# Two short runs of unread TensorE products in a hybrid decoder layer: while the first tokens load, and between the two products of the feed forward

## The chip, the cores and the metric

The kernel runs on one core of a Trainium2 chip. The metric is the device time of one execution in microseconds (us). Engines are named as in the profile: PE is TensorE, DVE is VectorE, ACT is ScalarE, POOL is GpSimd, SP is the engine that issues most of the transfers.

## The reference, cut to what matters

```python
def reference(x, w_in, w_o, ..., w_up, w_down, ln2_g, ln2_b):    # x: 1024 tokens x 1024, float32
    proj = x @ w_in[l]
    q, k, v, iq, ik, iw, hq, hf, hi, hg = jnp.split(proj, _split_points(), axis=-1)
    ...
    att = dsa_attention(q, k, v, iq, ik, iw * idx_w_scale)       # top 256 keys of each query by the indexer
    hgo = hgrn2(hq, hf, hi, hg, lower_bounds[l], hg_norm_g[l])   # gated linear recurrence
    mix = jnp.concatenate([att, hgo], axis=-1) @ w_o[l]
    x = layer_norm(ALPHA * x + mix, ln1_g[l], ln1_b[l])
    h = jnp.square(jax.nn.relu(x @ w_up[l])) @ w_down[l]         # 1024 -> 4096 -> 1024
    x = layer_norm(ALPHA * x + h, ln2_g[l], ln2_b[l])
```

## The kernel before

Every large product is made at float32 precision out of three faster ones: both operands are split into a high part (ACT, L88) and the rest (DVE or POOL, L89), and `mm3` issues high x high, high x low and low x high (L123 to L125) into one PSUM bank. PSUM is cut into three groups of banks: "mm" (four), "tr" (two) and "ou" (two).

The order in which the program writes the work is not the order in which the engines do it. The kernel is built with a planner (`schedule_with_timeline_sim`, L39): it plays the instructions through against estimated durations and writes the queue of each engine from that. Each engine then takes its queue strictly in that order.

*The start.* `turn_x(t)` (L144 to L151) loads 128 tokens (`xn`, 512 KB), transposes them on PE in eight 128x128 steps (L150, against `ident`) into "tr" banks, and splits them into `XH` and `XL`. The loads of tokens 0 and 1 are issued first, then four loads of the first weights (`wraw`, 324 columns), then the other tokens. The first products that mean something (`natural`, for the indexer, 128x324) follow from these tokens and weights. SBUF tiles `score[0..5]` (the indexer's scores) are reserved here, and first written much later by DVE.

*The middle.* Projections, the top-k search on DVE (`reach`, L313, and its rounds), the recurrence (`hgrn_unit`), attention, the output projection and the first layer norm.

*The feed forward.* Both products are done by a scheme of seven products for eight blocks. The first one runs over `NP` = 16 pairs of column blocks: `start_pair` issues two of a pair's seven `product`s and `end_pair` five, and the results go to memory (`hs`, `hd`). After the last `end_pair` the pools of the first product are closed, and the second product takes their place in SBUF: `down_w` and `down_h` load `rb` (weights) and `rs` (the stored results) and split them into `tw` and `sh`; `down_chunk` multiplies them (L123 to L125 with `tw`, `sh`), and DVE adds each finished bank to `acc` (L1072, L1074). SBUF is handed over tile by tile (`reuse_waits="tile"`): a load may start when the last reader of the tile that lay there is done.

Of the kernel before, what the change touches and what calls it, by code (L numbers as in the profile page):

```python
# [21 lines left out]
P = 128  # L22
# [20 lines left out]
def layer(ctx, tc, x, w_in, w_o, lb_logits, hg_norm_g, ln1_g, ln1_b, w_up, w_down, ln2_g, ln2_b,  # L43
          rope_tab, turn_tab, ident_c, causal_c, level_c, block_c, out, probe=None):
    nc = tc.nc
    PE, ACT, DVE, POOL = nc.tensor, nc.scalar, nc.vector, nc.gpsimd

    def dma(dst, src):
        return nc.sync.dma_start(dst, src)  # L49
# [18 lines left out]
    def bank(tag, bufs, shape=(P, 512), name="ps"):  # L68
        return psum.tile(list(shape), F32, name=name, tag=tag, bufs=bufs)

    def mm_bank(shape=(P, 512)):
        return bank("mm", 4, shape)

    def tr_bank(shape=(P, 4, P)):
        return bank("tr", 2, shape)
# [4 lines left out]
    ident = base.tile([P, P], F32, name="ident")  # L80
# [5 lines left out]
    def split_out(hi, lo, src, eng=None):  # L86

        first = ACT.activation(hi, src, AF.Copy)  # L88
        (eng or DVE).tensor_tensor(lo, src, hi.bitcast(F32), op=OP.subtract)  # L89
        return first  # L90
# [31 lines left out]
    def mm3(ps, ah, al, bh, bl, first, last, **kw):  # L122
        PE.matmul(ps, ah, bh, start=first, stop=False, **kw)  # L123
        PE.matmul(ps, ah, bl, start=False, stop=False, **kw)  # L124
        PE.matmul(ps, al, bh, start=False, stop=last, **kw)  # L125


    XH = [xt_tile(), xt_tile()]
# [4 lines left out]
    score = [s_pool.tile([P, P * (3 + j)], F32, name=f"score{j}") for j in range(6)]  # L133
# [10 lines left out]
    def turn_x(t):  # L144
        xn = xp.tile([P, DM], F32, name="xn", bufs=5)
        dma(xn, x[t * P:(t + 1) * P, :])
        for g in range(2):
            ps = tr_bank()
            for i in range(4):
                PE.transpose(ps[:, i], xn[:, (4 * g + i) * P:(4 * g + i + 1) * P], ident)  # L150
            split_out(XH[t // 4][:, t % 4, 4 * g:4 * g + 4, :], XL[t // 4][:, t % 4, 4 * g:4 * g + 4, :], ps)  # L151
# [7 lines left out]
    def natural(segs, evac, ws=None):  # L159

        n = sum(b - a for a, b in segs)
        ws = ws or in_weights(segs)
        for pr in range(4):
            ps = [mm_bank((P, n)) for _ in range(2)]
            for k in range(NK):
                w = ws[k // 2]
                for i in range(2):
                    t = 2 * pr + i
                    mm3(ps[i], XH[t // 4][:, t % 4, k, :], XL[t // 4][:, t % 4, k, :],
                        w[:, 0, k % 2, :], w[:, 1, k % 2, :], k == 0, k == NK - 1)  # L170
            for i in range(2):
                evac(2 * pr + i, ps[i])
            yield

    def turned(c0, dst):

        ws = [weight([rows(w_in, c0, c0 + 512, 2 * kp, 2)], [2, 512], 1, halves=True) for kp in range(4)]
        for g in range(2):
            for i in range(2):
                ps = [mm_bank() for _ in range(2)]  # L180
                for k in range(NK):
                    w = ws[k // 2]
                    for b in range(2):
                        sl = slice((2 * b + g) * P, (2 * b + g + 1) * P)
                        mm3(ps[b].rearrange("p (t n) -> p t n", t=4), w[:, 0, k % 2, sl], w[:, 1, k % 2, sl],
                            XH[i][:, :, k, :], XL[i][:, :, k, :], k == 0, k == NK - 1)
                n = slice(i * 512, (i + 1) * 512)
                for b in range(2):
                    u = kq.tile([P, 512], F32, name="ru", bufs=2)
                    v = kq.tile([P, 512], F32, name="rv", bufs=2)  # L190
                    DVE.tensor_tensor(u, ps[b], tab[:, 0, n], op=OP.mult)
                    DVE.tensor_tensor(v, ps[1 - b], tab[:, 1, n], op=OP.mult)
                    POOL.tensor_tensor(u, u, v, op=OP.add if b else OP.subtract)
                    parts = kq.tile([P, 2, 512], F32R, name="rparts", bufs=2)
                    split_out(parts[:, 0], parts[:, 1], u)
                    for j in range(2):
                        dma(dst[j, 4 * g:4 * g + 4, b, :, n], parts[:, j].bitcast(F32))
                yield
# [17 lines left out]
    first, irs = [], {}  # L216
# [23 lines left out]
    def turn_idx(t):  # L240
# [4 lines left out]
        if t >= 2:  # L245
# [4 lines left out]
            ACT.activation(iqs[:, :, sq], tp, AF.Copy)  # L250
            DVE.tensor_tensor(iqs[64:, :, sq], tp[64:], iqs[64:, :, sq].bitcast(F32), op=OP.subtract)

    turn_x(0)
    turn_x(1)
    ws = in_weights([(CI, CI + NI)], 2, xp)
# [541 lines left out]
    last = pairs[3]["last"]  # L797
# [48 lines left out]
    BX = {}  # L846
# [31 lines left out]
    for half in range(2):  # L878
        cs_ = slice(half * 512, half * 512 + 512)
        ws = [weight([rows(w_o, half * 512, half * 512 + 512, 2 * kp, 2)], [2, 512], 1, after=last) for kp in range(4)]  # L880
        for prt in range(4):
            ps = [mm_bank() for _ in range(2)]
# [23 lines left out]
    for tt in range(4):  # L906
        a, b = X1[tt], X1[tt + 4]
# [14 lines left out]
    def weights(p):  # L922
        r = raw_up(p, 2 * P)
        if p >= PRE:
            first_weights(p, r)
        a11, a12, a21, a22 = r[:, :4, :P], r[:, 4:, :P], r[:, :4, P:], r[:, 4:, P:]
        s = [upp.tile([P, 4, P], F32, name="ws", bufs=4) for _ in range(4)]
        DVE.tensor_tensor(s[0], a21, a22, op=OP.add)
        DVE.tensor_tensor(s[1], s[0], a11, op=OP.subtract)
        wq_split(p, "s2", s[1])  # L930
        wq_split(p, "s1", s[0])
        DVE.tensor_tensor(s[2], a11, a21, op=OP.subtract)
        wq_split(p, "s3", s[2])
        DVE.tensor_tensor(s[3], a12, s[1], op=OP.subtract)
        wq_split(p, "s4", s[3])
        wq_split(p, "22", a22)

    def product(ps, p, a, b, first):

        w = wq.pop((p, a))  # L940
        for k in range(4):
            mm3(ps, w[:, 0, k], w[:, 1, k], BX[b][:, 0, k], BX[b][:, 1, k], first and k == 0, k == 3,
                skip_group_check=True)

    def copied(ps):
        e = upp.tile([P, 512], F32, name="e", bufs=4)
        ACT.activation(e, ps, AF.Copy)
        return e
# [4 lines left out]
    def h_tile():  # L953
        return upp.tile([P, 512], F32, name="h", bufs=9)

    def keep(p, name, h):
        c = next(i for i, r in enumerate(CHUNKS) if p in r)
        ACT.dma_start(hs_d[c][ORDER.index(name), p - CHUNKS[c][0]], h)

    def block(p, i, j, ps, e=None):  # L960

        h = h_tile()
        if e is not None:
            DVE.tensor_tensor(h, ps, e, op=OP.add)
        ACT.activation(h, ps if e is None else h, AF.Relu)
        ACT.activation(h, h, AF.Square)
        if p in PLAIN:
            ACT.dma_start(hd[p][i * P:(i + 1) * P, j * 512:(j + 1) * 512], h)
            return
        name = f"a{j + 1}{i + 1}"  # L970
        hb[p, name] = h
        if name != "a21":
            keep(p, name, h)
        sums = {"a21": (("s1", "a21", "a22", OP.add), ("s2", "s1", "a11", OP.subtract), ("s3", "a11", "a21", OP.subtract)),
                "a12": (("s4", "a12", "s2", OP.subtract),)}
        for n, x1, x2, op in sums.get(name, ()):
            hb[p, n] = h_tile()
            DVE.tensor_tensor(hb[p, n], hb[p, x1], hb[p, x2], op=op)
            keep(p, n, hb[p, n])

    def start_pair(p):
        X = mm_bank()
        product(X, p, "11", "11", True)
        e1 = copied(X)
        Y = ou_bank()
        product(Y, p, "12", "21", True)
        block(p, 0, 0, Y, e1)
        held[p] = X

    def end_pair(p):  # L990
        X = held.pop(p)
        product(X, p, "s2", "t2", False)
        e2 = copied(X)
        Z = mm_bank()
        product(Z, p, "s1", "t1", True)
        e5 = copied(Z)
        product(X, p, "s3", "t3", False)
        block(p, 1, 1, X, e5)
        product(Z, p, "s4", "22", False)
        block(p, 0, 1, Z, e2)  # L1000
        product(X, p, "22", "t4", False)
        block(p, 1, 0, X)

    for p in range(PRE):
        start_pair(p)
    for p in range(NP):
        weights(p)
        if p >= PRE:
            start_pair(p)
        end_pair(p)  # L1010
    es_v.close()
    es_u.close()
    es_c.close()
# [101 lines left out]
    for t in range(NT):  # L1115
        ts = slice(t * P, (t + 1) * P)
        for gs in G:
            ps = mm_bank()
# [47 lines left out]
```

## Time and profile before

| | us |
|---|---|
| median of 3 runs | 1383.96 (1382.64 to 1385.42) |
| the profiled execution | 1383.45 |
| its span, first to last instruction | 1381.70 |
| PE busy | 1310.3 (95%) |
| DVE busy | 968.9 (70%) |
| ACT busy | 594.3 (43%) |
| POOL busy | 371.4 (27%) |

The mean granted clock of PE is 0.976 of full speed. PE's share is high nearly throughout; what matters are the few stretches where it is not. The records of matmuls have ends that are modelled, and they overlap: the distance from one start to the next says how fast PE goes, not the length of a record.

### The profile page before, as it was taken

The numbers are of one execution on the slowest core, as the hardware profiler recorded it, in microseconds if no ns is written. First come the engines' busy times: TensorE is split into PE (matmuls) and PEld (weight loads), VectorE is DVE, ScalarE is ACT, GpSimd is POOL, SyncE is SP. The second block draws the span as 40 slices with busy tenths as digits, with TensorE's granted clock in tenths as the row PEclk, the third lists the DMA queues.
The fourth block names the chain that finished last, engine by engine and source line by source line (L and its number), as shares of the span: only waits on it lengthen the run. The fifth ranks groups of instructions, "written<-read, shape, count | busy, mean of one in ns | idle before, by whom it ended". The sixth has DMA issues, their size and how long they took to land. (4 is left out here: it accounts for less than half of the span.)

```text
span 1381.7 us, 20797 instructions
## 1 busy us (share of the span) xinstructions
PE 1310.3 (95%) x7961; PEld 1067.1 (77%) x7961; DVE 968.9 (70%) x1821; ACT 594.3 (43%) x1038; POOL 371.4 (27%) x344
## 2 busy tenths in 40 slices
PE   8999799889899999999998999999998899999996
PEld 8877678677679956667887888888886688888875
DVE  4557989999993345553378755566537999887568
ACT  3333346655522455562135655555545343333131
POOL 3433302434515201132482000000003442341016
PEclk9999899999999999999999999999999999999998
DMA  5333322101103294106322544434466554443123
GB/s 219 111 101 104 101 57 61 45 20 32 48 32 92 72 192 99 36 31 199 128 99 79 176 145 160 160 130 151 154 213 240 187 196 149 157 160 92 54 100 122
DMA packets 96948, 162.50 MB, mean 118 GB/s; under 512 B 5832, under 2 KB 41040, under 8 KB 96720
## 3 DMA queue, kind: packets, MB, share of 16 engines
q1 hardware_dynamic: 81584, 133.37, 31.1%
q10 hardware_dynamic: 15264, 27.79, 5.7%
q8 instruction: 63, 1.03, 0.3%
q14 instruction: 37, 0.30, 0.1%
HBM read 114.48 MB, written 46.66 MB: 117 GB/s over the span
## 5 line engine op out<-in xcount | busy, mean ns | idle before, releaser
L123 PE MATMUL ps<-tw,sh 128*128 128x512 f32 x392 | 154.3, 396 | 8.5 <-ACT tw L88 5.1
L123 PE MATMUL ps<-w,xt 128*128 128x512 f32 (+2 forms) x448 | 158.4, 358 | 3.1 <-ACT HI L430 1.8
L125 PE MATMUL ps<-w,xt 128*128 128x512 f32 (+2 forms) x448 | 159.1, 356 | 0.0
L124 PE MATMUL ps<-w,xt 128*128 128x512 f32 (+2 forms) x448 | 158.9, 356 | 0.0
L124 PE MATMUL ps<-tw,sh 128*128 128x512 f32 x392 | 154.4, 394 | 1.5 <-DVE tw L89 1.5
L125 PE MATMUL ps<-tw,sh 128*128 128x512 f32 x392 | 153.0, 394 | 0.2 <-DVE sh L89 0.2
L89 POOL TENSOR_TENSOR w<-wraw,w 128x1024 fp32r<-128x1024 f32 (+2 forms) x46 | 95.5, 2087 | 118.5 <-ACT w L88 115.7
L1052 POOL TENSOR_TENSOR tt<-rb,rb 128x1536 f32<-128x1536 f32 (+1 forms) x5 | 19.6, 3912 | 392.1 <-DVE tw L89 314.7
L1074 DVE TENSOR_TENSOR acc<-acc,ps 128x512 f32<-128x512 f32 x140 | 92.0, 678 | 35.6 <-PE ps L125 35.5
L88 ACT ACTIVATE sh<-rs 128x1536 fp32r<-128x1536 f32 (+1 forms) x35 | 49.1, 1403 | 151.6 <-PE ps L125 141.7
L123 PE MATMUL ps<-xt,w 128*128 128x512 f32 x256 | 102.9, 402 | 0.0
L313 DVE TENSOR_SCALAR_CACHE_REDUCE junk<-score,cand 128x384 uint8<-128x384 f32 (+1 forms) x124 | 100.4, 810 | 2.7
L124 PE MATMUL ps<-xt,w 128*128 128x512 f32 x256 | 101.9, 398 | 0.0
L125 PE MATMUL ps<-xt,w 128*128 128x512 f32 x256 | 101.6, 397 | 0.0
L124 PE MATMUL ps<-xt,wq 128*128 128x512 f32 x256 | 99.9, 390 | 0.0
L123 PE MATMUL ps<-xt,wq 128*128 128x512 f32 x256 | 99.7, 390 | 0.0
L125 PE MATMUL ps<-xt,wq 128*128 128x512 f32 x256 | 99.6, 390 | 0.0
L345 ACT ACTIVATE sjunk<-score,scand 128x896 int8<-128x896 f32 (+1 forms) x62 | 67.8, 1094 | 69.5 <-DVE scand L355 53.5
L123 PEld LDWEIGHTS ps<-w,xt 128*128 128x128 f32 x448 | 86.0, 193 | 15.0 <-ACT HI L430 2.2
L124 PEld LDWEIGHTS ps<-w,xt 128*128 128x128 f32 x448 | 86.1, 192 | 11.5 <-issue 0.8
L123 PEld LDWEIGHTS ps<-tw,sh 128*128 128x128 f32 x392 | 75.0, 192 | 25.8 <-ACT tw L88 5.5
L125 PEld LDWEIGHTS ps<-w,xt 128*128 128x128 f32 x448 | 86.1, 192 | 10.4
(240 smaller groups left out, 3074.2 us busy)
## 6 DMA issues: line engine op xcount, KB each, us to landing
hs<-h ACTq DMA_DIRECT2D x98, 256.0 KB
rs<-hs SPq DMA_DIRECT2D x28, 768.0 KB
wr<-in_w_up_dram SPq DMA_DIRECT2D x16, 1024.0 KB
rb<-in_w_down_dram SPq DMA_DIRECT2D x16, 768.0 KB
wraw<-in_w_in_dram SPq DMA_DIRECT2D x20, 512.0 KB
ks<-kd SPq DMA_DIRECT2D x16, 512.0 KB
xn<-in_x_dram SPq DMA_DIRECT2D x8, 512.0 KB
kd<-rparts SPq DMA_DIRECT2D x16, 256.0 KB
```

What stands on the lines that cost most here:

```text
L88: first = ACT.activation(hi, src, AF.Copy)
L89: (eng or DVE).tensor_tensor(lo, src, hi.bitcast(F32), op=OP.subtract)
L123: PE.matmul(ps, ah, bh, start=first, stop=False, **kw)
L124: PE.matmul(ps, ah, bl, start=False, stop=False, **kw)
L125: PE.matmul(ps, al, bh, start=False, stop=last, **kw)
L313: DVE.tensor_scalar(junk[:, :wide[j]], score[j], at, 0.0, op0=op, op1=OP.add, accum_out=res)
L345: ACT.activation(sjunk[:, :wide[NB + j]], score[NB + j], AF.Sign, bias=0.0 if bias is None else bias[:, j:j + 1], scale=1.0, accum_out=cnt ...
L1052: POOL.tensor_tensor(t1, b12, b11, op=OP.subtract)
L1074: DVE.tensor_tensor(acc[t][:, gs], acc[t][:, gs], ps, op=OP.add)
```

## The change

A helper `keep_busy(n, m, after)` takes one "tr" bank and issues `n` products of a 128x128 float32 tile with itself. Nothing reads the bank. Each product is put behind `after` in the planner's order, without a wait of its own. It is called twice: with 8 products of a part of `score[0]`, which DVE fills with zeros for it, ahead of the first `turn_x`; and with 15 products of `ident` behind the last product of the first half of the feed forward. The other edits only return the last instruction, so that it can be named.

```diff
     def mm3(ps, ah, al, bh, bl, first, last, **kw):
         PE.matmul(ps, ah, bh, start=first, stop=False, **kw)
         PE.matmul(ps, ah, bl, start=False, stop=False, **kw)
-        PE.matmul(ps, al, bh, start=False, stop=last, **kw)
+        return PE.matmul(ps, al, bh, start=False, stop=last, **kw)
+
+    def keep_busy(n, m, after):
+
+        ps = tr_bank((P, P))
+        for _ in range(n):
+            r = PE.matmul(ps, m, m, start=True, stop=True)
+            tc.add_manual_dep(r.ins, after.ins.name, mybir.DependencyInfo(
+                mybir.DependencyClass.NoSync, mybir.DependencyReason.SCHED_ONLY), reason="place in the order")
...
+    keep_busy(8, score[0][:, :P], DVE.memset(score[0][:, :P], 0.0))
     turn_x(0)
     turn_x(1)
...
-        product(X, p, "22", "t4", False)
+        end = product(X, p, "22", "t4", False)
         block(p, 1, 0, X)
+        return end
...
-        end_pair(p)
+        end = end_pair(p)
+    keep_busy(15, ident, end)
     es_v.close()
```

## Rows read from the trace of the kernel before

**Rows 1.** Busy time and granted clock by stage (stretch, length, engines, PEclk, DMA share, GB/s).
```profile
4.75:11.20 6.45, 5.89 (x24) 5.40 (x25) 3.95 (x6) 4.82 (x8) 1.57 (x1) 1.00 1.03 382
11.20:30.00 18.80, 18.80 (x136) 18.75 (x136) 10.65 (x25) 5.48 (x13) 8.65 (x7) 1.00 0.60 224
...
200.00:390.00 190.00, 172.99 (x2124) 139.92 (x2123) 185.81 (x546) 104.91 (x210) 76.45 (x116) 0.96 0.14 39
...
740.00:1039.10 299.10, 299.10 (x1306) 244.92 (x1305) 178.70 (x275) 160.66 (x279) 0.00 (x0) 1.00 0.47 157
```

**Rows 2.** Instructions of PE in order of time, start of the kernel.
```profile
4.75 1.94 PE L150 MATMUL ps<-ident,xn 128*128 128x128 f32 x8 [4.75 <-DMA xn<-in_x_dram]
...
9.17 0.62 PE L124 MATMUL ps<-w,xt 128*128 128x324 f32 x1
...
11.21 0.36 PE L124 MATMUL ps<-w,xt 128*128 128x324 f32 x1
11.41 0.31 PE L125 MATMUL ps<-w,xt 128*128 128x324 f32 x1
11.56 0.31 PE L123 MATMUL ps<-w,xt 128*128 128x324 f32 x1
...
15.70 1.03 PE L150 MATMUL ps<-ident,xn 128*128 128x128 f32 x8
```

**Rows 3.** All engines in order of time, start of the kernel.
```profile
0.79 0.10 DVE L341 MEMSET need<- 128x1 f32 x2 [0.79 <-PEq L1155]
...
5.88 0.60 ACT L88 ACTIVATE xt<-ps 128x512 fp32r<-128x512 f32 x1 [3.88 <-PE ps L150]
6.50 0.69 DVE L89 TENSOR_TENSOR xt<-ps,xt 128x512 fp32r<-128x512 f32 x1 [5.62 <-ACT xt L88]
...
8.01 0.83 DVE L89 TENSOR_TENSOR w<-wraw,w 128x648 fp32r<-128x648 f32 x1
...
10.40 0.74 ACT L88 ACTIVATE w<-wraw 128x648 fp32r<-128x648 f32 x1
```

**Rows 4.** One line's durations (minimum, median, maximum in ns).
```profile
L150 PE MATMUL ps<-ident,xn x64: 270/273/474, 4.8 to 40.1; 128*128 128x128 f32 x64
```

**Rows 5.** PE in order of time: four float32 products, recorded as eight passes.
```profile
521.38 1.05 PE L751 MATMUL ps<-ident,wide 128*128 128x128 f32 x8
```

**Rows 6.** PE in order of time between the two products of the feed forward.
```profile
1038.73 0.39 PE L125 MATMUL ps<-xt,wq 128*128 128x512 f32 x1
1044.19 2.08 PE L123 MATMUL ps<-tw,sh 128*128 128x512 f32 x4 [5.07 <-ACT tw L88]
```

**Rows 7.** Busy time and granted clock there, columns as in rows 1.
```profile
1039.10:1042.20 3.10, 0.01 (x1) 0.00 (x0) 0.25 (x1) 2.28 (x3) 0.00 (x0) 0.99 0.73 246
1042.20:1044.20 2.00, 0.01 (x1) 0.01 (x1) 1.01 (x2) 1.06 (x1) 0.00 (x0) 0.50 0.86 293
1044.20:1049.00 4.80, 4.80 (x11) 3.80 (x12) 2.98 (x3) 1.06 (x1) 1.78 (x1) 0.50 1.04 394
1050.80:1094.10 43.30, 38.14 (x153) 29.77 (x152) 43.30 (x36) 20.66 (x18) 24.76 (x7) 0.92 0.61 207
1081.00:1086.30 5.30, 5.28 (x12) 4.15 (x13) 5.30 (x5) 1.76 (x2) 2.70 (x1) 0.50 0.49 148
```

**Rows 8.** The chain of waits there (start us, us, what ran or was waited for).
```profile
1039.14 0.38 SPq L49
...
1041.99 9.05 DMA rs<-hs
...
1089.90 4.15 DVE sh L89
...
1094.09 0.50 PE ps L125
1094.59 0.23 PE ps L123
```

**Rows 9.** From the page: a costly group of DVE (count, busy us, mean ns).
```profile
L313 DVE TENSOR_SCALAR_CACHE_REDUCE junk<-score,cand 128x384 uint8<-128x384 f32 (+1 forms) x124 | 100.4, 810 | 2.7
```

More of the change, by code (lines that the diff above doesn't have):

```diff
@@ L941, in product @@
         for k in range(4):
-            mm3(ps, w[:, 0, k], w[:, 1, k], BX[b][:, 0, k], BX[b][:, 1, k], first and k == 0, k == 3,
-                skip_group_check=True)
+            r = mm3(ps, w[:, 0, k], w[:, 1, k], BX[b][:, 0, k], BX[b][:, 1, k], first and k == 0, k == 3,
+                    skip_group_check=True)
+        return r
     def copied(ps):
```

## The prediction

> **What bounds the kernel now.** I read the busy time and clock by stage first. From 11.2 to 30 us PE is busy all of the time, and again over 299 us from 740 to 1039; in the stretch from 200 to 390 us DVE is the fuller engine, 185.8 us of 190 [rows 1]. So time that PE gains in the first microseconds reaches the end if what comes after is released by PE's own work. Then I read PE in order of time at the start. Its first instruction waits 4.75 us for the first tokens. After that it runs at half rate: seven starts of 128x324 products lie between 9.17 and 11.21, 0.29 us each, and then the distance falls to 0.15 us [rows 2]. [...] The transposes agree: eight at 4.75 take 1.94 us and eight at 15.70 take 1.03 us [rows 2].
>
> At the second place PE starts its last product of the first half at 1038.73 and waits 5.07 us from its end to 1044.19 [rows 6]. The clock is granted in full to about 1042.2, half from there to 1049.0; in that half-rate stretch eleven 128x512 products start in 4.80 us, 0.436 us each, against 0.23 us in the chain later [rows 7, 8]. But the chain of waits here does not run over PE. It goes from SP's issue at 1039.14 over the load of the stored results (9.05 us) and then, among DVE's splits and additions, to a last split that ends at 1094.05, for which PE waits at 1094.09 [rows 8]. DVE is busy 43.30 of 43.30 us from 1050.8 to 1094.1, PE only 38.14 [rows 7]. The reader is to see two places with the same symptom, a slow PE, and a different engine on the path.
>
> **The eight products at the start.** What they cost: a float32 product is recorded as two passes; eight passes took 1.05 us at the full clock [rows 5], the last record about 0.27, so (1.05 - 0.27)/7 = 0.111 us a pass. At half rate the transposes give the price: (1.94 - 0.47)/7 = 0.21 us a record, the last one being the longest of its line [rows 2, 4]. Sixteen passes take 3.4 to 3.6 us. They wait for the zeros: DVE's first instruction starts at 0.79, and DVE is idle until 6.50 [rows 3], so the fill is hidden there; I estimate 0.2 to 0.3 us for it from the small fill of 0.10 us, and a start at 1.1 to 1.2 us. They end at 4.5 to 4.8, against 4.75 when the tokens are in. Delay: 0 to 0.1 us.
>
> What they give: from PE's first work to the rise of the clock it took 6.45 us at the start (4.75 to 11.2) and 4.8 and 5.3 us in the two slow stretches later [rows 2, 7]. From 1.15 that puts the rise at 6.0 to 7.6 us instead of 11.2. Up to 11.14 ACT sets the pace, not PE: it is busy 4.82 us of the stretch's 6.45 and its conversions run from 5.88 to the one at 10.40, nearly without a gap [rows 1, 3]. So faster transposes bring nothing. The products after them gain. DVE has the low part of the first weights at 8.84 [rows 3]; the product at 9.17 could start at 8.9, and the seven to 11.21 would take 7 x 0.15 = 1.05 in place of 2.04 us [rows 2]. That is 1.0 + 0.27 = 1.3 us at most. Some of these products, in a fixed order, will stand for a low part that POOL or DVE has not yet made, so I take 0.9 us. The bounds are 0 (the clock does not rise, or the inputs hold PE) and 1.3; half of PE's 5.89 busy us would be 2.9, and ACT's fill excludes that. The next thing in the way is the second pair of token tiles: their transposes at 15.70 show no wait [rows 2], so the loads were in; that they were in 0.9 us earlier is not shown, and if not the gain ends there. I carry 0.9 us to the end, as PE is full to 30 us and the later stages hang on its products.
>
> **The fifteen products.** Thirty passes of 0.111 us are 3.3 us: from 1039.1 to 1042.4, before 1044.19, when PE's next operand is ready [rows 5, 6]. They are hidden by that wait, with 1.7 us to spare. If the clock were down they would take 6.3 us and end at 1045.4, 1.2 us too late. PE's idle time falls from 5.07 to 1.7 us, and the clock had held for some 3 us after the last product [rows 7], so I expect it to stay up: PE gains 11 x 0.2 = 2.2 us by 1049. What is late next is the load: DVE's full stretch begins when the stored results have landed and ACT has converted them, and it ends the wait at 1094.09. So I carry 0 of the 2.2 us; bounds 0 and 2.2, nearer 0 by the row in which DVE has no idle time at all. The loads are issued when the last real product ends; the fifteen read only `ident` and write a bank, so they hold up none of them. A second slow stretch, from 1081 to 1086 [rows 7], follows a wait for DVE and stays.
>
> **The other edits** return a value and cost nothing. The sum: 1383.45 - 0.9 - 0 = 1382.55 for the profiled execution. The median of the runs shown lies 0.51 above it, so 1383.96 - 0.9 = 1383.1. About 0.2% (2.8 us) is what a measurement here can tell from no change, and this is a third of it.
>
> **Rivals.**
>
> *The second place pays as well.* If the planner now puts three of DVE's four additions of the first product ahead of the split at 1050.8, in the time in which DVE waits for the load, PE's 2.2 us are kept: 0.9 + 2.2 = 3.1, 1380.9. For it: PE and DVE end within 0.1 us of each other at 1094 [rows 8]. Against it: DVE's order must change, for which I see no cause there.
>
> [...]
>
> *The planner's order turns out dearer.* All queues are written by playing the whole program through; the trace shows that this moves work far (fills that the program writes in the middle run at 0.79 [rows 3]). Eight products at the start and fifteen later shift that play. The place where it costs most is the stretch from 200 to 390 us, where DVE is full: a round of the search, four counts of 0.81 us [rows 9], put ahead of a step that PE waits for, costs 3.2 us. One such round gives 1383.1 + 3.2 = 1386.3, two 1389.5; it decides from 2.8 + 0.9 = 3.7 us, a little more than one round. For it: nothing keeps the order fixed. Against it: the shift is small.
>
> *The planner's order turns out cheaper*, by the same round: 1383.1 - 3.2 = 1379.9.
>
> **How the numbers follow.** My forecast has 0.40, the unraised clock 0.14, both within 0.2%. The second place paying has 0.20 and the cheaper order 0.11, both faster; the dearer order has 0.15, of which I count 0.13 as slower. That makes faster 0.31, same 0.56, slower 0.13. The range goes from the cheaper order with some of the second place's gain (1379.3) to one dear round (1386.5); the likeliest case's own range is 1382.5 to 1384.1.
>
> **What would show it.** Right: sixteen passes before the first transpose, which still starts within 0.1 us of 4.75; 128x324 products 0.15 us apart before 9.5 us; the transposes of 15.70 at about 14.8; the clock at 1.00 from 1039 to 1077 and thirty passes in the gap; DVE's full stretch and PE's wait at its end about where they were, counted from the last real product. Wrong: distances of 0.27 us to 11 us; the first `sh`-and-`tw` stretch ending over 1 us sooner after that product; or a gap between the two traces that grows in the middle of the kernel, where neither place lies.

## The result, and the profile after

| | median, us | ratio to before (95% interval) |
|---|---|---|
| before, on the same chip | 1382.64 (1380.52 to 1387.16) | |
| the change | 1375.37 (1372.3 to 1378.3, and one of 2953.8) | 0.9942 [0.992, 0.9964] |
| the change once more, with profile | 1376.68 (1372.89 to 1378.61) | 0.9946 [0.9928, 0.9964] |

The kernel is faster by some 7 to 8 us. 1383.1 was forecast, with a range from 1379.3: the direction that had got 0.31 came true, with eight to nine times the gain forecast, and the range missed it. The profiled execution of the change took 2953.8 us, over twice the others; the ratio leaves it out, and the profile of the third row is shown, with a span of 1376.7 us.

By stage, columns as in [rows 1], which these rows answer:

```profile
4.75:11.20 6.45, 5.03 (x26) 4.51 (x26) 3.13 (x5) 3.96 (x7) 1.49 (x1) 1.00 1.04 392
11.20:30.00 18.80, 18.80 (x137) 18.75 (x136) 11.20 (x25) 6.51 (x16) 8.77 (x8) 1.00 0.63 233
200.00:390.00 190.00, 174.20 (x2192) 140.87 (x2190) 183.16 (x553) 104.95 (x209) 76.75 (x116) 0.95 0.15 40
734.00:1033.00 299.00, 299.00 (x1307) 245.14 (x1306) 177.79 (x275) 160.78 (x280) 0.00 (x0) 1.00 0.46 157
```

In the same 190 us from 200 on, PE has 68 more records than before and DVE seven more: the program gets further in the same time, so it gains on the way. In a stretch where PE is full, 740 to 1039 before and 734 to 1033 here, nothing is gained.

PE in order of time at the start, against [rows 2]:

```profile
1.04 3.78 PE L131 MATMUL ps<-score 128*128 128x128 f32 x16 [1.04 <-DVE need L350]
5.69 1.94 PE L158 MATMUL ps<-ident,xn 128*128 128x128 f32 x8 [0.87 <-DMA xn<-in_x_dram]
8.19 1.11 PE L158 MATMUL ps<-ident,xn 128*128 128x128 f32 x4 [0.56 <-DVE xt L89]
...
10.00 0.39 PE L124 MATMUL ps<-w,xt 128*128 128x324 f32 x1
10.23 0.31 PE L125 MATMUL ps<-w,xt 128*128 128x324 f32 x1
10.38 0.31 PE L123 MATMUL ps<-w,xt 128*128 128x324 f32 x1
...
15.57 1.03 PE L158 MATMUL ps<-ident,xn 128*128 128x128 f32 x8
```

The sixteen passes are there and done at 4.82. In this execution the tokens came 0.94 us later than before. The four transposes at 8.19 take 1.11 us, as long as the same four took before:

```profile
7.25 1.11 PE L150 MATMUL ps<-ident,xn 128*128 128x128 f32 x4 [0.56 <-DVE xt L89]
```

So PE is not yet at its later rate there: with the first call alone the four take 0.68 us (experiment 1). At the start I read the clock from this rate, as my estimate; the column of the granted clock says 1.00 from 4.75 to 11.20 in both traces. The products are 0.15 us apart from 10.23, not from 11.2, and the transposes of 15.70 stand at 15.57.

PE between the two products of the feed forward, against [rows 6]; then busy time and clock there, against [rows 7]:

```profile
1032.67 0.40 PE L125 MATMUL ps<-xt,wq 128*128 128x512 f32 x1
1032.91 3.51 PE L131 MATMUL ps<-ident 128*128 128x128 f32 x30
1038.11 1.20 PE L123 MATMUL ps<-tw,sh 128*128 128x512 f32 x4 [1.69 <-ACT tw L88]
```

```profile
1038.00:1043.00 5.00, 4.82 (x20) 3.69 (x21) 3.05 (x3) 1.12 (x2) 1.89 (x1) 1.00 1.04 397
1044.70:1088.00 43.30, 37.48 (x147) 29.40 (x147) 43.30 (x36) 21.78 (x19) 25.16 (x7) 0.92 0.60 206
```

The chain of waits there ends as in [rows 8]:

```profile
1083.88 4.06 DVE sh L89
1087.98 0.50 PE ps L125
```

The clock stays at 1.00 over the first of these rows, PE makes twenty products in 5.0 us where it made eleven in 4.8, and DVE is busy 43.30 of 43.30 us all the same. From the start of the last real product to the end of the wait for DVE it is 1087.98 - 1032.67 = 55.31 us, before 1094.09 - 1038.73 = 55.36.

**Where the time went.** I matched the instructions of ACT and DVE of the two traces one by one and took the difference of their starts, in us against before:

| at (before's time) | the change | first call alone | second call alone | order alone |
|---|---|---|---|---|
| 31 | -0.1 | -0.6 | +0.2 | -0.3 |
| 200 | -1.0 | -2.2 | -1.7 | -1.1 |
| 245 | -4.8 | -6.3 | -1.7 | -1.1 |
| 430 to 500 | -2.2 | -6.1 | +0.5 | -0.8 |
| 520 to 1038 | -6.7 to -6.1 | -10.5 | +0.3 to +0.4 | -0.5 |
| 1100 | -6.1 | -10.3 | +0.6 | -0.5 |

Two steps carry it: some 4 us between 200 and 245, and 4.5 us between 500 and 520. Neither lies where the change is. The smaller steps (at 190 us, where DVE waits 0 to 2.1 us for a load, and around 300) come and go between executions.

### The profile page after: what moved, and what is told of

Its sections match the earlier page's. It is cut to its first block, busy times and chain, and to the rows that moved or that the text cites. A ratio compares the mean times of both kernels' runs of the same rounds, so it can differ in the third digit from the quotient of the medians.

```text
span 2952.0 us, 20890 instructions
## 1 busy us (share of the span) xinstructions
PE 2940.2 (100%) x8007; PEld 1883.7 (64%) x8007; DVE 927.1 (31%) x1822; ACT 600.0 (20%) x1038; POOL 351.4 (12%) x344
## 3 DMA queue, kind: packets, MB, share of 16 engines
q1 hardware_dynamic: 81584, 133.37, 14.5%
## 4 chain that ended last, share of the span: by engine, by line
PE 100%; DVE 0%; ACT 0%; POOLq 0%; POOL 0%; DVEq 0%; issue 0%
PE ps L124 27%; PE ps L123 27%; PE ps L125 27%; PE ps L745 3%; PE ps L719 3%; PE ps L700 2%; PE ps L491 2%; PE ps L701 2%; PE ps L865 1%; PE ps L542 1%; PE ps L292 1%; PE ps L291 1%; PE ps L760 1%; PE ps L158 1%; PE ps L528 1%; PE ps L544 1%
## 5 line engine op out<-in xcount | busy, mean ns | idle before, releaser
L125 PE MATMUL ps<-w,xt 128*128 128x512 f32 (+2 forms) x448 | 321.2, 718 | 0.0
L124 PE MATMUL ps<-w,xt 128*128 128x512 f32 (+2 forms) x448 | 318.5, 713 | 0.0
L123 PE MATMUL ps<-w,xt 128*128 128x512 f32 (+2 forms) x448 | 317.0, 714 | 0.0
L124 PE MATMUL ps<-tw,sh 128*128 128x512 f32 x392 | 265.4, 677 | 0.0
L123 PE MATMUL ps<-tw,sh 128*128 128x512 f32 x392 | 264.8, 679 | 0.0
L125 PE MATMUL ps<-tw,sh 128*128 128x512 f32 x392 | 264.0, 678 | 0.0
L123 PE MATMUL ps<-xt,w 128*128 128x512 f32 x256 | 212.5, 830 | 0.0
L124 PE MATMUL ps<-xt,w 128*128 128x512 f32 x256 | 211.8, 827 | 0.0
L125 PE MATMUL ps<-xt,w 128*128 128x512 f32 x256 | 211.1, 825 | 0.0
L125 PEld LDWEIGHTS ps<-w,xt 128*128 128x128 f32 x448 | 169.8, 379 | 62.5 <-issue 59.4
L124 PEld LDWEIGHTS ps<-w,xt 128*128 128x128 f32 x448 | 167.9, 375 | 64.6 <-issue 61.2
L123 PEld LDWEIGHTS ps<-w,xt 128*128 128x128 f32 x448 | 167.1, 374 | 61.7 <-issue 54.9
L124 PE MATMUL ps<-xt,wq 128*128 128x512 f32 x256 | 178.4, 697 | 0.0
L123 PE MATMUL ps<-xt,wq 128*128 128x512 f32 x256 | 177.7, 694 | 0.0
L125 PE MATMUL ps<-xt,wq 128*128 128x512 f32 x256 | 177.7, 696 | 0.0
L123 PEld LDWEIGHTS ps<-tw,sh 128*128 128x128 f32 x392 | 117.0, 299 | 66.3 <-issue 59.9
L124 PEld LDWEIGHTS ps<-tw,sh 128*128 128x128 f32 x392 | 116.3, 297 | 66.3 <-issue 61.3
L125 PEld LDWEIGHTS ps<-tw,sh 128*128 128x128 f32 x392 | 115.6, 295 | 67.3 <-issue 62.6
L89 POOL TENSOR_TENSOR w<-wraw,w 128x1024 fp32r<-128x1024 f32 (+2 forms) x46 | 89.5, 1955 | 319.8 <-ACT w L88 289.4
L125 PEld LDWEIGHTS ps<-xt,w 128*128 128x128 f32 x256 | 90.1, 352 | 56.3 <-issue 54.3
```

What stands on the lines that cost most here:

```text
L125: return PE.matmul(ps, al, bh, start=False, stop=last, **kw)
```

## Experiments

Each was timed in five rounds against the kernel before on the same chip. Where it says that the queues are pinned, the kernel is planned once, the order of each queue is recorded, and the kernel that runs takes that order over, with only the named instructions added.

**1. The calls apart, and the order alone.** The first call alone; the second alone; and no products, but the queues as the planner wrote them with both calls.

```diff
# first call alone
-    keep_busy(15, ident, end)
# second call alone
-    keep_busy(8, score[0][:, :P], DVE.memset(score[0][:, :P], 0.0))
# order alone: planned with both calls, run with neither
+PLANNED_WITH, RUN_WITH = ['first', 'second'], []
```

> The change itself once more, for a profile at the usual speed. The sum of the prediction (0.9 us from the start, 0 from the gap between the two products) would give a ratio of 0.999; a ratio near 0.994 says that some 7 us come from somewhere that it did not count. The second place pays: the first product of the second half runs 0.23 us a matmul and DVE's chain behind it ends 2 us or more sooner, counted from the last product of the first half. The start pays more: the distance between the traces is already several us before 740 us.

> Only the eight products at the start. If the start's worth is its own 0.9 us: ratio 0.999. If the gain of some 8 us comes from the start and what hangs on it (fewer stretches at the half clock in the middle): 0.994 to 0.996. If the second place pays: no more than 0.999.

> Only the fifteen products between the two halves of the feed forward. If DVE's full stretch hides what PE gains: 1.000. If PE's 2.2 us are kept: 0.998. If this place carries the whole result: 0.994 to 0.996. If the fifteen hold up what comes behind them: above 1.001.

> No unread products at all, but each engine's queue in the order that the planner wrote with them (it differs from the old one only in the first 20 us: on ACT and DVE a token tile's conversion goes ahead of a weight's, on PE some of the first products are swapped). If the planner's order is what pays: 0.994 to 0.996. If the products themselves do: 1.000 within 0.001.

First call 0.9929 [0.9905, 0.9953] (1373.92 us), second call 0.9998 [0.9979, 1.0017], order 1.0001 [0.9985, 1.0017]. All of the gain belongs to the first call, and to the products, not to the order. PE at the start with the first call alone:

```profile
1.04 3.78 PE L131 MATMUL ps<-score 128*128 128x128 f32 x16 [1.04 <-DVE need L350]
4.66 1.94 PE L158 MATMUL ps<-ident,xn 128*128 128x128 f32 x8
7.16 0.68 PE L158 MATMUL ps<-ident,xn 128*128 128x128 f32 x4 [0.56 <-DVE xt L89]
8.60 0.42 PE L123 MATMUL ps<-w,xt 128*128 128x324 f32 x1 [0.76 <-ACT w L88]
...
15.09 1.03 PE L158 MATMUL ps<-ident,xn 128*128 128x128 f32 x8
```

Four transposes take 0.68 us at 7.16, where they took 1.11 at 7.25 before: by PE's rate the clock is up by then. The transposes of 15.70 stand at 15.09, 0.6 us sooner. That is no more than executions differ. In the run with a transfer at 210 us (experiment 4), which puts nothing ahead of the tokens, the four are at half rate and the later ones come sooner still:

```profile
7.21 1.11 PE L166 MATMUL ps<-ident,xn 128*128 128x128 f32 x4 [0.56 <-DVE xt L95]
...
14.77 1.03 PE L166 MATMUL ps<-ident,xn 128*128 128x128 f32 x8
```

In the six traces without a product at the start (before, order alone, second call, eight late, eight in the middle, transfer at 210) these transposes stand at 14.77 to 15.92, and the first two products 0.15 us apart at 9.4 to 11.6. So the earlier clock is shown and time gained by it is not; at any rate the other 9 us are not from here.

**2. The same number of instructions without the clock; the same time with fewer instructions.** Queues pinned to the order before. Eight products of 32x32 at the start; then two of 128x512; then four of 32x32; and eight of 32x32 at 453 us, ahead of the second half of the gate products.

```diff
+    keep_busy(8, score[0][:, :32], score[0][:, :32], DVE.memset(score[0][:, :32], 0.0))
# instead: keep_busy(2, score[1][:, :P], score[1], DVE.memset(score[1], 0.0))
# instead: keep_busy(4, ...) of the 32x32
# instead, ahead of g1 = gates(1, ...): twice keep_busy(4, ident[:, :32], ident[:, :32])
```

> The eight products are made 32x32, so that they take well under 1 us and leave the clock as it was; they are as many instructions as before, at the same place, and all queues stand in the order of the kernel before. If the place of PE's instruction fetches is what pays (each brings 16 KB, some 256 instructions; more instructions at the start move all later fetches to earlier times, into the load at 211 us and out of the load at 489 us): ratio 0.993 to 0.996. If the clock at the start pays: 1.000.

> Two products of 128x512 in place of eight of 128x128, the old order: PE is as busy before the tokens as with the eight, with a quarter of the instructions. If the clock at the start and what hangs on it pays: 0.993 to 0.995. If the place of the fetches pays: the start gains some 0.5 us, the fetches move by about a quarter as far, the stretches at 211 to 250 us and at 489 to 510 us stay as before: 0.9995 to 1.000.

> Four 32x32 products at the start, the old order. If the place of the fetches pays, by half the shift: the fetch of 219 us comes near 216, at the end of the load, and the one of 489 us about 483, still within its load: 0.997 to 1.000, the load at 489 us not helped. If the clock at the start pays: 1.000.

> Eight 32x32 products, not at the start but ahead of the second pair of gate products (after 400 us), the old order. If the place of the fetches pays: nothing changes at 211 to 250 us; the fetch at 489 us moves ahead, PE's wait for the keys at 504 us falls from 2.9 us to about 1 and the clock stays up there: 0.997, some 4 us. If the start is what pays, in whatever way: 1.000.

Eight small ones: 0.9952 [0.9935, 0.9969], though PE's rate comes up no sooner there:

```profile
7.49 1.12 PE L162 MATMUL ps<-ident,xn 128*128 128x128 f32 x4 [0.56 <-DVE xt L91]
...
10.09 0.47 PE L127 MATMUL ps<-w,xt 128*128 128x324 f32 x1
10.36 0.47 PE L125 MATMUL ps<-w,xt 128*128 128x324 f32 x1
10.63 0.39 PE L126 MATMUL ps<-w,xt 128*128 128x324 f32 x1
```

The transposes still take 1.12 us and the products come 0.27 us apart to 10.6. Four small ones: 0.9998 [0.9981, 1.0015]. Two long ones: 0.9977 [0.9962, 0.9992], between the two outcomes that I had named; by PE's rate the clock is up there (four transposes at 7.49 take 0.66 us), and whether that is what gains is open. Eight in the middle: 0.9987 [0.9974, 1.0], less than the 0.997 expected: by the matching above, its trace gains 4.5 us at 500, but falls back 3.7 us from 400 to 460 and 1.9 us behind 1320. Most of the gain needs no earlier rise of the clock at the start, and it depends on how many instructions are put in. One thing that moves with their number is the place of the instruction fetches: near 210 us one comes 7.2 us behind the first issue of a load before, 3.2 us with four small products and 1.5 us with eight (last table). The page of before lists fetches as a queue of their own (packets, MB, share):

```profile
q8 instruction: 63, 1.03, 0.3%
```

That is 63 packets of 16 KB, 1.07 us each on average. That they are PE's is my estimate: the page counts 7961 matmuls and as many weight loads, some 253 to a packet, and products, with one fill of zeros, are all that the runs with moved fetches add.

In the trace of the DMA queues, the stretch from the first issue of the weights' load near 210 us, 4.97 us before and then 5.20 us with the first call alone:

```profile
q1 hardware_dynamic: 1088, 0.52, 41.3%
```

```profile
q1 hardware_dynamic: 1088, 0.52, 41.9%
q8 instruction: 1, 0.02, 1.5%
```

The extra instructions have moved a fetch into the load, 1.1 us behind its first issue. All engines in order of time, before:

```profile
215.93 1.06 ACT L88 ACTIVATE w<-wraw 128x1024 fp32r<-128x1024 f32 x1 [0.38 <-DMA wraw<-in_w_in_dram]
...
217.12 2.39 POOL L89 TENSOR_TENSOR w<-wraw,w 128x1024 fp32r<-128x1024 f32 x1 [0.16 <-ACT w L88]
217.21 2.33 DVE L355 TENSOR_SCALAR scand<-scur 128x2 int32<-128x2 int32 x1
...
223.95 2.39 POOL L89 TENSOR_TENSOR w<-wraw,w 128x1024 fp32r<-128x1024 f32 x1 [4.43 <-ACT w L88]
...
224.22 2.15 DVE L355 TENSOR_SCALAR scand<-scur 128x2 int32<-128x2 int32 x1
```

and in the change:

```profile
216.14 0.17 DVE L364 TENSOR_SCALAR scand<-scur 128x2 int32<-128x2 int32 x1
216.35 1.06 ACT L88 ACTIVATE w<-wraw 128x1024 fp32r<-128x1024 f32 x1 [1.86 <-DMA wraw<-in_w_in_dram]
216.43 0.61 DVE L322 TENSOR_SCALAR_CACHE_REDUCE junk<-score,cand 128x384 uint8<-128x384 f32 x1
...
217.54 2.40 POOL L89 TENSOR_TENSOR w<-wraw,w 128x1024 fp32r<-128x1024 f32 x1 [1.65 <-ACT w L88]
...
217.88 0.88 DVE L322 TENSOR_SCALAR_CACHE_REDUCE junk<-score,cand 128x640 uint8<-128x640 f32 x1
```

Before, a DVE step on two columns, 0.17 us in the change, starts 0.09 us after POOL's split and takes 2.33 us, until POOL is done. It happens a second time at 224.22 (2.15 us). In the change ACT waits longer for the load, POOL's split starts later, and DVE is by then in its counts, which run beside POOL undisturbed (0.88 us at 217.88, as at 221.09 before, where POOL does nothing). Two times some 2 us: the step of 4 us. The later load makes the kernel faster. Why a step on two columns waits for POOL's split and a count does not (2.33 us against 0.88) was not shown.

The second step: PE near 500 us, before, with its clock row, then with the first call alone:

```profile
503.79 0.45 PE L691 MATMUL ps<-ks,qs 128*128 128x128 f32 x1 [2.85 <-DMA ks<-kd]
```

```profile
503.70:509.60 5.90, 5.81 (x21) 3.72 (x21) 1.60 (x9) 2.52 (x10) 0.43 (x2) 0.50 0.36 77
```

```profile
495.89 0.30 PE L700 MATMUL ps<-ks,qs 128*128 128x128 f32 x1 [1.09 <-DMA ks<-kd]
```

```profile
495.80:501.70 5.90, 5.80 (x39) 4.57 (x41) 2.76 (x12) 2.45 (x11) 0.42 (x2) 1.00 0.65 136
```

The attention's keys land 1.8 us sooner after the load's first issue, and PE's granted clock does not fall behind the shorter wait, 1.00 after 1.09 us against 0.50 after 2.85: 39 matmuls in the 5.9 us that held 21.

**3. More of them, and later.** 12, 16 and 24 products of 32x32 at the start, and eight ahead of the scores of the last pair of heads (574 us), queues pinned. The two places should now come apart.

> Twelve products of 32x32 at the start, every queue else as before. The traces so far: near 210 us the fetch of PE's instructions that comes 1.1 to 2.1 us after the issue of the weights' load goes with a gain of some 4 us, one at 3.2 us or later (none, two or four products) with none; near 480 us a fetch 1.8 to 2.3 us ahead of the load's first issue goes with a gain of 4.5 us, one at +0.4 to +9.3 us with none. Theory (place of the fetch): twelve move the first fetch to about the issue of the load or ahead of it (-1.5 to +0.5 us), so the gain at 210 us is lost, and the second stays ahead of its load, so the gain at 480 us is kept: ratio 0.9955 to 0.9975. Rival (more instructions, or something at the start, gain by themselves): as eight or better, 0.9952 or below, with both gains.

> Sixteen products of 32x32 at the start, every queue else as before; they fit the wait for the tokens (eight took 1.77 us of its 4.75). Theory (place of the fetch): the fetch near 210 us falls 2 us or more ahead of the weights' load, no gain there; the one near 480 us stays ahead of its load and the next one is not yet in its first 10 us, so 4.5 us are gained there: 0.9955 to 0.9975. Rival (dose): more gain than with eight, under 0.995.

> Twenty-four products of 32x32 at the start, every queue else as before; by the 0.22 us of one of eight they take 5.3 us, about 0.6 us more than the wait that holds them. Theory (place of the fetch): no gain near 210 us; near 480 us the fetch after the one that was ahead of the load comes some 16 us after the load's first issue, or, held up, later: gain kept if it is behind the issue of the keys (at +9.9 us), lost if ahead of it: 0.9965 or 1.0005, and which of the two goes with where the trace shows the fetch. Rival (dose): under 0.995.

> Eight products of 32x32 before the scores of the last pair of heads, after both places of the gain, every queue else as before. Theory (place of the fetch): none of the two gains, and eight products cost at most 1.3 us in a stretch that TensorE fills: 0.9995 to 1.001. Rival (the number of instructions, wherever they stand): 0.995.

12: 0.996 [0.9943, 0.9978]. 16: 0.9973 [0.9955, 0.999]. 24: 0.9989 [0.9974, 1.0004]. Late: 1.001 [0.9995, 1.0025]. Twenty-four gain less than eight, and eight late ones nothing: the number by itself is not the cause. For 16 I had expected no gain at 210 us, and its trace has one (last table). They all fit the wait for the tokens: 24 are done at 3.71 us, not the 5.3 that I had reckoned.

**4. The transfer without the products.** A useless transfer of 256 KB (memory to memory) in the queue of SP: behind the first issue of the load at 210 us, with no products anywhere; and, with eight small products at the start, ahead of the keys or behind them at 480 us. Queues pinned.

```diff
+block = dma(dram.tile([16, 4096], F32, name="block"), w_up[0:16])   # at the named place in SP's queue
```

> No products at all; every queue is that of the kernel before but for one useless transfer of 16 rows of 16 KB (256 KB, memory to memory), issued behind the first issue of the weights' load near 212 us. Theory (a fetch inside this load holds it up, ACT's second conversion and so POOL's split come later and miss DVE's small steps): ACT's second conversion starts 4.9 to 6 us after the first issue in place of 3.9, POOL's split 6 us or more after it, and a kernel with MORE to do is 4 us faster: 0.996 to 0.998. Rival (the gain at 210 us has to do with TensorE's instructions themselves, and the load is only beside it): 1.000 to 1.002.

> The eight products of 32x32 at the start (0.9952 alone), and one useless transfer of 256 KB issued between the load of the values and the issue of the keys near 480 us. Theory (what stands ahead of the keys in the transfers' queues decides): the keys land 1 us or more later, TensorE waits 2 us or more in place of 0.9 and its clock goes to half: the gain of 4.6 us there is lost, 0.9980 to 0.9995. Rival (the gain there is of TensorE's instructions and not of the load): 0.9945 to 0.996.

> As the run before, but the transfer is issued behind the keys. Theory: the keys land as without it, gain kept: 0.9945 to 0.9965. If any further 256 KB in this stretch cost the same, wherever they stand in the queue: 0.998 to 0.9995.

At 210 us: 0.9975 [0.9959, 0.9991]; the kernel that has only MORE to do is 3.5 us faster. Its rows, all engines in order of time:

```profile
215.82 0.17 DVE L373 TENSOR_SCALAR scand<-scur 128x2 int32<-128x2 int32 x1
...
215.94 1.06 ACT L94 ACTIVATE w<-wraw 128x1024 fp32r<-128x1024 f32 x1 [1.77 <-DMA wraw<-in_w_in_dram]
...
217.13 2.41 POOL L95 TENSOR_TENSOR w<-wraw,w 128x1024 fp32r<-128x1024 f32 x1 [1.56 <-ACT w L94]
```

They are those of the change, with no product of it. This trace also gains 3.4 us at 500, which the transfer was not meant to touch, so the ratio is not the price of the place at 210 alone. At 480 us my expectation failed: ahead of the keys 0.9946 [0.9929, 0.9963], behind them 0.9936 [0.9914, 0.9958], both with the gain. The transfer ahead of the keys moved their last packet by only 0.2 us (21.3 us after the load's first issue, against 21.1 with eight small products alone).

**All traces side by side.** Times are in us after the first issue of the load (of weights near 210, of the output weights, queries, values and keys near 480), from the starts and ends of packets and instructions; the gains are the steps between 200 and 245 and between 500 and 520.

| run | 210: fetch | ACT's second conversion | gain | 480: fetch | last value packet | PE has the keys | gain |
|---|---|---|---|---|---|---|---|
| before | 7.2 | 3.89 | | 9.3 | 13.6 | 24.3 | |
| order alone | 6.7 | 3.88 | 0 | 8.8 | 13.1 | 24.5 | -0.2 |
| second call | 6.0 | 3.89 | 0 | 4.7 | 13.0 | 24.3 | 0.1 |
| two long | 3.9 | 3.90 | 0 | 9.1 | 13.7 | 25.1 | -1.0 |
| four small | 3.2 | 3.87 | 0 | 0.4 | 14.5 | 25.3 | -1.3 |
| eight, late | 5.9 | 3.84 | 0 | 4.3 | 12.1 | 23.1 | 2.3 |
| transfer at 210 | 6.9 | 5.28 | 3.4 | 8.8 | 12.5 | 23.6 | 3.4 |
| 24 small | -6.2 | 3.89 | 0 | -6.1, 18.8 | 11.3 | 23.1 | 2.4 |
| 16 small | -2.5 | 4.10 | 4.1 | -4.0, 21.0 | 11.5 | 22.5 | 4.4 |
| 12 small | -0.9 | 3.87 | 0 | -3.1 | 11.3 | 22.4 | 4.5 |
| eight, middle | 6.0 | 3.94 | -0.1 | -1.8 | 11.7 | 22.5 | 4.5 |
| eight small | 1.5 | 5.06 | 4.0 | -2.2 | 11.5 | 22.4 | 4.6 |
| first call | 1.1 | 4.86 | 4.1 | -2.3 | 11.4 | 22.6 | 4.4 |
| the change | 2.1 | 5.37 | 3.7 | -2.2 | 11.6 | 22.4 | 4.5 |
| ahead of keys | 1.0 | 5.03 | 4.1 | -2.3 | 11.2 | 22.4 | 4.5 |
| behind keys | 2.7 | 5.39 | 3.7 | -2.1 | 11.5 | 22.4 | 4.6 |

Near 210, ACT's conversion at 3.94 or before goes with no gain, at 4.10 or later with 3.4 to 4.1 us: an edge, not a slope. The run with 16 stands just over it with a fetch ahead of the load, so a fetch is one way over the edge and not the only one. The edge is DVE's short step: POOL's split starts 1.2 us behind the conversion, and DVE comes to the step 5.15 to 5.17 us into the load. In the runs with no gain POOL has started by then, at 5.03 to 5.14 us; in those with a gain it starts at 5.29 to 6.58. (With eight late ones POOL starts at 5.03 and holds up the step before that one, for 2.40 us.) Near 480, every trace with a fetch 0 to 9.3 us into the load has its last value packet at 12.1 to 14.5 and the keys at 23.1 to 25.3; those with a fetch ahead of the load and none in its first 20 us have 11.2 to 11.7 and 22.4 to 22.6. The lag is that of a few packets: of the 1024 of the values, 20 to 42 end over 0.3 us behind the 960th in the seven traces with a fetch 0 to 9.3 us into the load, and none or one in the others (14 with eight in the middle). Each row is one execution, and single executions of one kernel differ by several us (1378.28 to 1390.22 for before in experiment 4), so a row's gains are not its median's: the run with 12 gained 4.5 us at 480 in its trace and lost part of it elsewhere.

## Why the prediction was wrong

**The clock at the start: it rose sooner in one trace of the two; the 0.9 us are not shown.** The products began at 1.04 (forecast 1.15). With the first call alone the transposes started at 4.66, and the clock was up by 7.2 (forecast 6.0 to 7.6), as it was by 7.5 with the two long products; in the profiled change, whose tokens came late, it was not up at 8.19. For 0.9 us forecast, the transposes of 15.70 came 0.6 us sooner with the first call alone and 0.13 in the change; executions without the products have them from 0.9 us sooner to 0.2 us later. The forecast took the rise at 11.2 from the distances of products in one trace, and in the six without a product at the start it lies anywhere from 9.4 to 11.6. With the first call alone ACT's conversion of the weights held the first product until 8.60, as the text feared of the inputs. The unraised clock, which had 0.14, fell there and is open for the change. With the first call alone the rate had doubled at 7.16, with nothing but transposes and a wait since 4.82; whether the rise goes with the unread products or with the transposes, no run tells.

**The second place: right.** Thirty passes take 3.51 us (forecast 3.3) and leave 1.69 idle (1.7); the clock stays up; DVE's chain keeps the whole of it, 55.31 us against 55.36. Alone it gives 0.9998. The rival in which it pays fell.

**The planner's order, dearer or cheaper: both fell.** Order alone gives 1.0001. The cheaper one named the right stretch, 200 to 390 us, and about the right sum for it, by luck: no queue there has another order.

**The step that failed** is "I carry 0.9 us to the end, as PE is full to 30 us and the later stages hang on its products". It takes the rest of the kernel as something that a gain passes through unchanged, unless a queue's order changes. The sum had no term for the instructions themselves that the eight products add ahead of everything: they shift all later instruction fetches (PE's, by my estimate) against the loads, while the loads keep their place in the work. In the change a fetch came 2.1 us after the first issue of the load near 210 us (before 7.2), and one came 2.2 us ahead of the load near 480 us (before 9.3 after). The text did say what would show it: a gap between the traces that grows in the middle, where neither place lies. It grew by 3.7 us at 210 and 4.5 at 500.

**How far the cause is shown.** At 210 us it is: a transfer inside that load, with no products at all, gives the same rows and 0.9975. That a fetch does to this load what the transfer does is read side by side: with a fetch 1.0 to 2.7 us into it, ACT's conversion stands at 4.86 to 5.39, with one later or ahead of the load (the transfer apart) at 3.84 to 4.10. That DVE's small steps wait out POOL's split is read from rows, in which both end together (before, at 219.54 and 219.51, and at 226.37 and 226.34). At 480 us the link from fetch to keys is shown only side by side, in sixteen traces; the run that was to make it by hand moved its 256 KB as 16 packets of 16 KB and cost the keys 0.2 us, so it did not reproduce the lag. A fetch is a single packet of 16 KB, and by what it would make the last value packet up to 3 us late, and 20 to 42 of the 1024, was not shown. What is given back behind 1320 us (0.6 to 1.9 us in most runs) was not followed.

**The fastest version** is the first call alone, 1373.92 us, 0.9929 [0.9905, 0.9953]; its interval overlaps that of the change.

## What to carry to other kernels

When a small edit gives more than its own place can, match the two traces instruction by instruction and look for the stretch in which the gap grows; then run a control with the same number of useless instructions. A gain of this kind is an accident of where fetches, loads and short DVE steps meet: the next edit can lose it, as 24 products in place of eight do. What lasts would be to remove the sensitivity itself: to keep POOL's splits off DVE's smallest steps, or to load the keys earlier. Neither was tried. In the trace of before, 25 DVE steps on two or four columns between 130 and 400 us take 0.35 to 2.40 us beside a POOL instruction, 29.2 us together, where one alone takes 0.17.

## What the runs showed of the hardware

- A DVE step on 128x2 that takes 0.17 us alone took 2.33 and 2.15 us when it started within 0.3 us of the start of a POOL split of 2.39 us; counts of 128x640 and 128x768 beside such a split kept their 0.88 and 1.01 us.
- The trace of before has 63 packets of 16 KB in its queue for instructions, 1.07 us each on average. With one of them in the first 10 us of a load of 5.8 MB, PE had the keys in it at 23.1 to 25.3 us, with none in its first 20 us at 22.4 to 22.6.
- A wait of 1.09 us in attention left the granted clock at 1.00, one of 2.85 us was followed by 5.9 us at 0.50. The wait alone does not decide: with the transfer at 210 us one of 2.07 us left 1.00, with eight late products one of 1.63 us was followed by 0.71.
- A useless transfer of 256 KB made the kernel faster by 0.25% (0.9975 [0.9959, 0.9991]), with DVE's step and POOL's split no longer meeting.
